# A running log-sum-exp kernel: weights marked as held, four loads up front, and a last store cut into 5, 75 and 48 partitions

The kernel runs on one core of a Trainium2 chip. The metric is the device time of one execution in microseconds (us), as the median of several executions of the same program; lower is better.

## The reference

For `x` of shape (4, 4096, 4128), float32, the output is a running log-sum-exp along the second axis:

```python
out[:, 0, :] = x[:, 0, :]
for t in range(1, S):
    mx = np.maximum(out[:, t - 1, :], x[:, t, :])
    out[:, t, :] = mx + np.log(np.exp(out[:, t - 1, :] - mx) + np.exp(x[:, t, :] - mx))
```

270.5 MB are read and as many written.

## The kernel before

The rows of a batch are taken in steps of 384 (R = 3 rows on each of 128 partitions), and one step of 256 per batch. A step is loaded whole, goes through ACT (Exp), PE (triangular matmuls that form prefix sums, plus the carry) and ACT (Ln), and is stored whole. Steps are cut into four column chunks, and the chunks of successive steps are interleaved on the engines. Cut to what the change and the argument touch:

```python
    def mm(pt, w, rhs, start=False, stop=False):
        nc.tensor.matmul(pt, lhsT=w, rhs=rhs, start=start, stop=stop, skip_group_check=True)
    ...
        def load(self):
            full = xpool.tile([P, R, D], FP32, name="xt")      # bufs = 4
            ...
            nc.sync.dma_start(out=self.xt, in_=self.dram(x))

        def store(self):
            nc.sync.dma_start(out=self.dram(out), in_=self.xt)
    ...
        def head(self):
            ...
            for j in range(t.r):
                for s in range(0, CH, MM):
                    mm(pt[:, s:s + MM], excl if j else incl, self.e(j, s, s + MM), start=j == 0)
            ...
    ahead = bufs - 1
    for s in steps[:ahead]:
        s.load()
    ...
    for g in range(len(chunks) + R - 1):
        for d in range(R - 1, -1, -1):
            if 0 <= g - d < len(chunks) and d < chunks[g - d].t.r:
                k = chunks[g - d]
                k.stage(d)                       # Ln of row d, then the matmuls of row d + 1
                if k.c == last and d + 1 == k.t.r:
                    k.t.store()
                    if stored + ahead < len(steps):
                        steps[stored + ahead].load()
                    stored += 1
        if g + 2 < len(chunks):
            chunks[g + 2].exp()
        if g + 1 < len(chunks):
            chunks[g + 1].head()
```

The softmax here doesn't subtract the row's maximum and nothing guards it: scores larger than these inputs give would overflow.

Of the kernel before, what the change touches and what calls it, by code (L numbers as in the profile page):

```python
# [10 lines left out]
P = 128  # L11
R = 3
CH = 1024
MM = 512
HI, LO = 96, 32


def _constants(nc, pool):


    def tri(base, name):
        t = pool.tile([P, P], FP16, name=name)
        nc.gpsimd.memset(t, 1.0)

        nc.gpsimd.affine_select(  # L25
            out=t, in_=t, pattern=[[1, P]], compare_op=mybir.AluOpType.is_ge,
            fill=0.0, base=base, channel_multiplier=-1,
        )
        return t

    def ones_where_zero(bases, step, name):
        t = pool.tile([P, P], FP16, name=name)
        nc.gpsimd.memset(t, 0.0)
        for base in bases:
            nc.gpsimd.affine_select(  # L35
                out=t, in_=t, pattern=[[step, P]], compare_op=mybir.AluOpType.not_equal,
                fill=1.0, base=base, channel_multiplier=1,
            )
        return t

    return (
        tri(0, "incl"),
        tri(-1, "excl"),
        ones_where_zero([0], -1, "ident"),
        ones_where_zero([-(HI + 31), -(LO + 31)], 0, "pick"),
    )


@with_exitstack
def kernel(  # L50
    ctx: ExitStack,
    tc: tile.TileContext,
    x: bass.AP,
    out: bass.AP,
):






    nc = tc.nc
    B, S, D = x.shape
    assert S % P == 0
    n_main = D // CH
    tail = D - n_main * CH
    t0 = n_main * CH
    last = n_main - 1

    nc.scalar.preload_act_table_set("natural_log_exp_and_others")  # L70
    consts = ctx.enter_context(tc.tile_pool(name="consts", bufs=1))
    incl, excl, ident, pick = _constants(nc, consts)

    bufs = 4
    xpool = ctx.enter_context(tc.tile_pool(name="xpool", bufs=bufs))
    cpool = ctx.enter_context(tc.tile_pool(name="cpool", bufs=1))
    pmain = ctx.enter_context(tc.tile_pool(name="pmain", bufs=3, space=bass.MemoryType.PSUM))
    ptail = ctx.enter_context(tc.tile_pool(name="ptail", bufs=2, space=bass.MemoryType.PSUM))

    carry = [cpool.tile([P, CH], FP16, name=f"carry{c}") for c in range(n_main)]  # L80
    carry_t = cpool.tile([P, tail], FP16, name="carry_t")
    for t in (*carry, carry_t):
        nc.vector.memset(t, 0.0)  # L83

    ctx.enter_context(tc.manual_schedule())

    def mm(pt, w, rhs, start=False, stop=False):
        nc.tensor.matmul(pt, lhsT=w, rhs=rhs, start=start, stop=stop, skip_group_check=True)  # L88

    def keep(cr, pt):  # L90

        nc.vector.tensor_copy(cr[HI:HI + 32, :], pt[HI:HI + 32])  # L92
        nc.vector.tensor_tensor(  # L93
            out=cr[LO:LO + 32, :], in0=pt[HI:HI + 32], in1=cr[HI:HI + 32, :],
            op=mybir.AluOpType.subtract,
        )

    class Step:


        def __init__(self, b, row, r):
            self.b, self.row, self.r = b, row, r
            self.first = row == 0

        def dram(self, t):
            rows = t[self.b, self.row:self.row + P * self.r, :]
            return rows.rearrange("(p j) d -> p j d", j=self.r)

        def load(self):
            full = xpool.tile([P, R, D], FP32, name="xt")  # L110
            self.xt = full[:, :self.r, :]
            self.half = self.xt.bitcast(FP16)
            nc.sync.dma_start(out=self.xt, in_=self.dram(x))  # L113

        def store(self):
            nc.sync.dma_start(out=self.dram(out), in_=self.xt)  # L116

    class Chunk:
        def __init__(self, step, c):
            self.t, self.c = step, c  # L120
            self.w = D - last * CH if c == last else CH

        def e(self, j, a, b):
            return self.t.half[:, j, 2 * self.c * CH + a:2 * self.c * CH + b]

        def exp(self):
            c0, w = self.c * CH, self.w
            nc.scalar.activation(  # L128
                self.t.half[:, :, 2 * c0:2 * c0 + w], self.t.xt[:, :, c0:c0 + w], ACT.Exp,
            )  # L130

        def head(self):
            t = self.t
            pt = self.pt = pmain.tile([P, CH], FP32, name="pt")
# [3 lines that stand above are left out]
            if not t.first:  # L138
                for s in range(0, CH, MM):
                    mm(pt[:, s:s + MM], pick, carry[self.c][:, s:s + MM])  # L140
            if self.c == last:
                self.tail_head()

        def tail_head(self):


            t, r = self.t, self.t.r
            full = ptail.tile([P, R, tail], FP32, name="qt")
            qt = self.qt = full[:, :r, :]
            to = lambda v, n: v.unsqueeze(1).to_broadcast([P, n, tail])  # L150
            for i in range(r):
                e = self.e(i, CH, CH + tail)
                mm(qt[:, i:, :], incl, to(e, r - i), start=i == 0)
                if i:
                    mm(qt[:, :i, :], excl, to(e, i))
            if not t.first:
                mm(qt, pick, to(carry_t, r))

        def stage(self, j):

            t, c, pt = self.t, self.c, self.pt
            nc.scalar.activation(t.xt[:, j, c * CH:(c + 1) * CH], pt, ACT.Ln)  # L162
            if j + 1 < t.r:
                for s in range(0, CH, MM):
                    mm(pt[:, s:s + MM], ident, self.e(j + 1, s, s + MM), stop=j + 2 == t.r)
                if c == last and j == 0:
                    nc.scalar.activation(t.xt[:, :, t0:D], self.qt, ACT.Ln)  # L167
                    keep(carry_t, self.qt[:, t.r - 1, :])
            else:
                keep(carry[c], pt)  # L170

    steps = []
    for b in range(B):
        n = S // P
        parts = [R] * (n // R) + ([n % R] if n % R else [])
        if b == 0:
            parts.reverse()
        row = 0
        for r in parts:
            steps.append(Step(b, row, r))  # L180
            row += P * r
        assert row == S

    chunks = [Chunk(s, c) for s in steps for c in range(n_main)]
    ahead = bufs - 1
    for s in steps[:ahead]:
        s.load()
    stored = 0
    chunks[0].exp()
    chunks[1].exp()  # L190
    chunks[0].head()
# [3 lines that stand above are left out]
                k = chunks[g - d]  # L195
                k.stage(d)
                if k.c == last and d + 1 == k.t.r:
                    k.t.store()
                    if stored + ahead < len(steps):
                        steps[stored + ahead].load()  # L200
                    stored += 1
        if g + 2 < len(chunks):
# [3 lines that stand above are left out]
# [30 lines left out]
```

## Time and profile before

| | before |
|---|---|
| time, median of the first 3 runs | 1262.91 us (1262.84 to 1263.04) |
| span of the profiled run | 1261.0 us |
| data queue, share of the 16 DMA engines' time | 99.4% |
| PE / weight loads / DVE / ACT busy | 55 / 19 / 36 / 75% |
| last load landed | 1220.69 us |
| last store: first packet starts, last packet ends | 1249.15, 1259.74 us |

The busy shares say what could be the bound, the chain of waits says what was at the end. Two things come from the packet records of the trace, which hold start, duration and size of every DMA packet: the duration of a packet, and which packets follow each other on one engine (the next starts a few ns before or after the last ends). The prediction below shows the other views.

### The profile page before, as it was taken

How to read it: one execution, taken by the hardware profiler on the slowest of the kernel's cores; microseconds unless marked ns; L12 is line 12 of the kernel's file. 1: busy time of each engine (PE TensorE's matmuls, PEld its weight loads, DVE VectorE, ACT ScalarE, POOL GpSimd, SP SyncE). 2: the span in 40 equal slices, each digit the busy share in tenths (PEclk: the TensorE clock that was granted, in tenths of full speed). 3: DMA queues.
4: the chain of work that ended last, by engine and by line, in shares of the span. 5: the costliest groups of instructions: out<-in, count | busy, mean ns of one | idle time of the engine just before them, and what ended most of it. 6: DMA issues, size and time to landing. Idle time of an engine off the chain costs nothing.

```text
span 1261.0 us, 6165 instructions
## 1 busy us (share of the span) xinstructions
PE 688.7 (55%) x2268; PEld 237.0 (19%) x2268; DVE 451.4 (36%) x445; ACT 947.3 (75%) x733; POOL 2.2 (0%) x13
## 2 busy tenths in 40 slices
PE   3665554555555555655346555555634755664552
PEld 1222111111121111211112211111211211221120
DVE  2443333333333333334424333333442433333344
ACT  5997777777777777778569777777966977777794
POOL 0000000000000000000000000000000000000000
PEclk9887777777677777777768777787777777778786
DMA  9999999999999999999999999999999999999998
GB/s 411 410 439 431 432 427 434 438 430 432 433 437 431 432 432 436 432 427 436 431 433 436 437 429 431 436 436 432 430 434 435 432 431 432 434 435 431 433 422 347
DMA packets 12702, 541.46 MB, mean 429 GB/s; under 512 B 1408, under 2 KB 1408, under 8 KB 1408
## 3 DMA queue, kind: packets, MB, share of 16 engines
q1 hardware_dynamic: 12672, 541.07, 99.4%
q8 instruction: 18, 0.29, 0.1%
q14 instruction: 12, 0.10, 0.0%
HBM read 270.53 MB, written 270.53 MB: 429 GB/s over the span
## 4 chain that ended last, share of the span: by engine, by line
DMA 69%; ACT 21%; PE 5%; issue 2%; DVE 1%; SPq 0%; ACTq 0%
DMA xt<-in_x_dram 67%; ACT xt L128 11%; ACT xt L162 10%; PE pt L88 5%; DMA out_dram<-xt 2%; ACT xt L167 0%; SPq L116 0%; DVE carry L92 0%; DVE carry L93 0%; ACTq L231 0%; SPq L113 0%; ACTq L128 0%; PE qt L88 0%
## 5 line engine op out<-in xcount | busy, mean ns | idle before, releaser
L128 ACT ACTIVATE xt<-xt 128x3072 f16<-128x3072 f32 (+3 forms) x176 | 478.5, 2719 | 247.9 <-DMA xt<-in_x_dram 247.8
L88 PE MATMUL pt<-xt,ident 128*128 128x512 f16 x672 | 251.3, 470 | 530.7 <-ACT xt L162 530.4
L162 ACT ACTIVATE xt<-pt 128x1024 f32<-128x1024 f32 x512 | 487.6, 1030 | 2.5 <-PE pt L88 0.7
L92 DVE CAST carry<-pt 32x1024 f16<-32x1024 f32 x176 | 216.4, 1230 | 761.0 <-ACT xt L162 760.7
L88 PE MATMUL pt<-xt,excl 128*128 128x512 f16 x672 | 247.0, 504 | 0.0
L93 DVE TENSOR_TENSOR carry<-pt,carry 32x1024 f16<-32x1024 f32 x176 | 215.9, 1227 | 6.1
L88 PEld LDWEIGHTS <-ident 128*128 128x128 f16 x672 | 70.1, 104 | 677.7 <-issue 654.0
L88 PE MATMUL pt<-xt,incl 128*128 128x512 f16 x352 | 152.0, 526 | 23.6 <-ACT xt L128 15.0
L88 PEld LDWEIGHTS <-excl 128*128 128x128 f16 x756 | 92.5, 124 | 141.0 <-issue 108.1
L88 PE MATMUL pt<-carry,pick 128*128 128x512 f16 x320 | 109.8, 429 | 0.0
L88 PEld LDWEIGHTS <-incl 128*128 128x128 f16 x480 | 45.2, 111 | 129.7 <-DVE carry L93 95.2
L88 PEld LDWEIGHTS <-pick 128*128 128x128 f16 x360 | 40.6, 113 | 57.0 <-issue 34.3
L167 ACT ACTIVATE xt<-qt 128x96 f32<-128x96 f32 (+1 forms) x44 | 10.9, 249 | 45.7 <-PE pt L88 45.7
L92 DVE CAST carry_t<-qt 32x32 f16<-32x32 f32 x44 | 8.7, 197 | 25.5 <-ACT xt L167 25.4
L88 PE MATMUL qt<-xt,incl 128*128 128x64 f16 (+2 forms) x128 | 12.3, 196 | 0.0
L88 PE MATMUL qt<-xt,excl 128*128 128x64 f16 (+1 forms) x84 | 10.6, 187 | 0.0
L93 DVE TENSOR_TENSOR carry_t<-qt,carry_t 32x32 f16<-32x32 f32 x44 | 8.5, 193 | 1.5
L88 PE MATMUL qt<-carry_t,pick 128*128 128x96 f16 (+1 forms) x40 | 8.2, 204 | 0.0
L83 DVE MEMSET carry<- 128x512 uint32 x4 | 1.9, 485 | 1.1 <-PEq L220 1.0
L70 ACT ACT_TABLE_LOAD x1 | 1.3, 1283 | 0.8 <-PEq L220 0.8
L35 POOL TENSOR_SCALAR_AFFINE_SELECT pick<-pick 128x128 f16<-128x128 f16 x2 | 0.6, 294 | 0.1
L25 POOL TENSOR_SCALAR_AFFINE_SELECT incl<-incl 128x128 f16<-128x128 f16 x1 | 0.3, 294 | 0.0
(11 smaller groups left out, 1.9 us busy)
## 6 DMA issues: line engine op xcount, KB each, us to landing
xt<-in_x_dram SPq DMA_DIRECT2D x40, 6192.0 KB, 42.2
out_dram<-xt SPq DMA_DIRECT2D x40, 6192.0 KB, 28.1
xt<-in_x_dram SPq DMA_DIRECT2D x4, 4128.0 KB, 37.3
out_dram<-xt SPq DMA_DIRECT2D x4, 4128.0 KB, 23.0
```

The lines of the kernel that those rows point to most:

```text
L25: nc.gpsimd.affine_select(out=t, in_=t, pattern=[[1, P]], compare_op=mybir.AluOpType.is_ge, fill=0.0, base=base, channel_multiplier=-1,)
L35: nc.gpsimd.affine_select(out=t, in_=t, pattern=[[step, P]], compare_op=mybir.AluOpType.not_equal, fill=1.0, base=base, channel_multiplier=1,)
L70: nc.scalar.preload_act_table_set("natural_log_exp_and_others")
L83: nc.vector.memset(t, 0.0)
L88: nc.tensor.matmul(pt, lhsT=w, rhs=rhs, start=start, stop=stop, skip_group_check=True)
L92: nc.vector.tensor_copy(cr[HI:HI + 32, :], pt[HI:HI + 32])
L93: nc.vector.tensor_tensor(out=cr[LO:LO + 32, :], in0=pt[HI:HI + 32], in1=cr[HI:HI + 32, :], op=mybir.AluOpType.subtract,)
L128: nc.scalar.activation(self.t.half[:, :, 2 * c0:2 * c0 + w], self.t.xt[:, :, c0:c0 + w], ACT.Exp,)
L162: nc.scalar.activation(t.xt[:, j, c * CH:(c + 1) * CH], pt, ACT.Ln)
L167: nc.scalar.activation(t.xt[:, :, t0:D], self.qt, ACT.Ln)
```

## The change

Three parts. First, a matmul whose stationary operand is the same as that of the matmul before it is to run without loading it again (`ldweights=False`), and the matmuls of the tail are put in an order that allows this more often. Second, all four buffers are loaded before the first store, in place of three. Third, the last store goes out as partitions 0-4, 5-79 and 80-127; the aim is that the fifth DMA engine, taken for the slow one, gets 4 packets of it and not 8.

```diff
--- before.py
+++ after.py
@@ -12,6 +12,9 @@
 R = 3
 CH = 1024
 MM = 512
+
+
+UNEVEN = ((0, 5), (5, 80), (80, P))
 HI, LO = 96, 32
 
 
@@ -84,8 +87,22 @@
 
     ctx.enter_context(tc.manual_schedule())
 
+    held = [None]
+
     def mm(pt, w, rhs, start=False, stop=False):
-        nc.tensor.matmul(pt, lhsT=w, rhs=rhs, start=start, stop=stop, skip_group_check=True)
+
+        if held[0] is not w:
+            nc.tensor.matmul(pt, lhsT=w, rhs=rhs, start=start, stop=stop, skip_group_check=True)
+            held[0] = w
+            return
+        pe = nc.tensor
+        pe.add_instruction(mybir.InstMatmult(
+            name=nc.get_next_instruction_name(),
+            ins=[pe.lower_ap(rhs), pe.lower_ap(w, for_matmul_weights=True)],
+            outs=[pe.lower_ap(pt, opt=True)],
+            start_tensor_calc=start, stop_tensor_calc=stop, ldweights=False,
+            tile_size=(P, P), tile_position=(0, 0), bass_skip_group_check=True,
+        ))
 
     def keep(cr, pt):
 
@@ -112,8 +129,9 @@
             self.half = self.xt.bitcast(FP16)
             nc.sync.dma_start(out=self.xt, in_=self.dram(x))
 
-        def store(self):
-            nc.sync.dma_start(out=self.dram(out), in_=self.xt)
+        def store(self, parts=((0, P),)):
+            for a, b in parts:
+                nc.sync.dma_start(out=self.dram(out)[a:b], in_=self.xt[a:b])
 
     class Chunk:
         def __init__(self, step, c):
@@ -149,10 +167,9 @@
             qt = self.qt = full[:, :r, :]
             to = lambda v, n: v.unsqueeze(1).to_broadcast([P, n, tail])
             for i in range(r):
-                e = self.e(i, CH, CH + tail)
-                mm(qt[:, i:, :], incl, to(e, r - i), start=i == 0)
-                if i:
-                    mm(qt[:, :i, :], excl, to(e, i))
+                mm(qt[:, i:, :], incl, to(self.e(i, CH, CH + tail), r - i), start=i == 0)
+            for i in range(1, r):
+                mm(qt[:, :i, :], excl, to(self.e(i, CH, CH + tail), i))
             if not t.first:
                 mm(qt, pick, to(carry_t, r))
 
@@ -183,7 +200,7 @@
 
     chunks = [Chunk(s, c) for s in steps for c in range(n_main)]
     ahead = bufs - 1
-    for s in steps[:ahead]:
+    for s in steps[:bufs]:
         s.load()
     stored = 0
     chunks[0].exp()
@@ -195,8 +212,8 @@
                 k = chunks[g - d]
                 k.stage(d)
                 if k.c == last and d + 1 == k.t.r:
-                    k.t.store()
-                    if stored + ahead < len(steps):
+                    k.t.store(UNEVEN if k.t is steps[-1] else ((0, P),))
+                    if bufs <= stored + ahead < len(steps):
                         steps[stored + ahead].load()
                     stored += 1
         if g + 2 < len(chunks):
```

## The prediction

> **What bounds the kernel now.** I read the page first, the DMA part before the engine part, then the chain of waits in its last 80 us, then the order of instructions on SP and ACT there.
>
> ```profile
> PE 688.7 (55%) x2268; PEld 237.0 (19%) x2268; DVE 451.4 (36%) x445; ACT 947.3 (75%) x733; POOL 2.2 (0%) x13
> ...
> DMA packets 12702, 541.46 MB, mean 429 GB/s; under 512 B 1408, under 2 KB 1408, under 8 KB 1408
> ...
> q1 hardware_dynamic: 12672, 541.07, 99.4%
> q8 instruction: 18, 0.29, 0.1%
> q14 instruction: 12, 0.10, 0.0%
> ```
>
> The data queue keeps the 16 DMA engines busy for 99.4% of the span; no compute engine is above 75%. 12672 packets are 88 transfers (44 loads, 44 stores) of 128 data packets, one per partition, and 16 completion writes. Each engine gets 8 data packets of each transfer. In the packet records a 49,536-byte packet takes 1.829 us and a 33,024-byte one 1.222 us, in nearly every case: 27 GB/s per engine, loads and stores alike. An engine therefore needs 8 x (80 x 1.829 + 8 x 1.222) = 1248.8 us of the 1261.0; successive packets overlap by 3 to 4 ns, 704 times, so about 1246. Nothing in the change takes a byte away. What can move is the other 15 us: the start, the places where an engine stands still, and the tail.
>
> Chaining packets (the next starts 3 to 4 ns before the last ends) gives 16 engine histories. They start at 1.8 to 2.4 us. One never stops and ends at 1259.74; the other 15 end at 1258.9 to 1259.1. The span ends 1.3 us after the last packet. Those 15 stood still once, before the next-to-last store:
>
> ```profile
> SPq L116 <- ACT xt L162: 1178.4, 44, 30.0
> ```
> ```profile
> 1183.04 37.65 DMA xt<-in_x_dram
> 1220.69 0.02 issue
> ...
> 1220.78 1.91 ACT xt L128
> 1222.68 2.75 ACT xt L162 x3
> ...
> 1225.48 0.61 PE pt L88 x2
> ...
> 1226.11 0.25 ACT xt L167
> 1226.36 1.80 ACT xt L128
> 1228.16 2.74 ACT xt L162 x3
> 1230.90 1.11 ACT xt L128
> ```
> ```profile
> DMA  9299949994979779472402021200920092009202
> ```
>
> SP issues a store only after the ACT work of its step, and ACT runs exponentials of the next step in between. So the next-to-last store waits for the last load, landed at 1220.69, plus 12.9 us of nearly gapless ACT work, and is issued at 1233.63. The DMA digits (1221 to 1240 us, 0.48 us each) show the engines running dry one after another from about 1228 and starting together near 1235. Then 8 packets of 1.829 and 8 of 1.222 us give 24.3 us, to 1259. The last store, issued at 1244.12, has about 5 us in hand. The end is thus set twice over: by the last load's landing on the *slowest* engine, and by that engine's own unbroken backlog.
>
> Why one engine is slow is in the landings. The 16 completions of the first load lie within 0.54 us, those of the last within 7.3 us (next slowest 6.2, then 4.6; mean about 2.9). The packet histories show one cause: the 16-KB instruction fetches of queue q8, 18 of them some 65 us apart, each landing on one engine and delaying it by about 1.5 us (a gap near 1.0 and a stretched packet near 0.45, for example at 59, 604 and 1101 us). The 8-KB ones cost about 0.6.
>
> [...]
>
> **The change, part by part.**
>
> *Held weights.* A three-block chunk has 12 matmuls in the order ident (4), incl (2), excl (4), pick (2), each preceded by a load; held, 4 loads remain. The tail chunk has 6 more matmuls, 3 more loads after the reordering. Per step 3 x 4 + 7 = 19 loads in place of 54; in all about 820 in place of 2268. PE is not the bound, so the 1450 loads at 0.11 us (160 us) are nearly all worth nothing. Two pieces are on the path. First, in the last chain ACT waits once for a pair of ident matmuls (0.61 us)[...]. Second, the program shrinks [...], so q8 goes from 18 fetches to 12 or 13. Five or six delays of 1.5 us over 16 engines are 0.5 us on average, but what counts is the slowest engine, whose lag contains two or three fetches: one fewer is 1.5 us, none fewer is 0, two fewer 3. I choose 1.5. It brings the last landing, the next-to-last store and the end forward by as much.
>
> *Four loads up front.* The fourth load was issued at 37.39, right behind the first store at 37.00; now it is before it. The rings held work until 42 us in both cases, and from the load of step 4 on the order of transfers is the same. Same bytes, no gap filled: 0. One oddity could pay: the last packets of the third load, at 40 us, took 2.5 to 3.2 us in place of 1.829 on all engines. If that is because the rings were nearly empty when the first store arrived, it goes, 1.1 us; if it belongs to the first store as such, it only moves. The last store also met a short queue (5 us) without such a packet, so I give it one in five: minus 0.2.
>
> *The last store in three.* Partitions 5, 75 and 48 run on 5, 15 and 16 engines with 1, 5 and 3 packets each. That the fifth engine gets 4 (1 + 3) is true only if a transfer's engines start where the last one's left off: the 75 then use all but the fifth. Engines one to four get 9, the rest 8. [...] Either way some engines carry 9 packets, 1.222 us more. They were ready at 1259.0, so they end at 1260.2 where the slowest ended at 1259.74: plus 0.5. If the fifth is the slow one, its 4 packets spare it 4.9 us, of which only the 0.74 by which it trails can be of use. Two more issues on SP (0.34 us each) fit into the 5 us in hand; two more completion writes of 9 ns are nothing.
>
> Sum: 0.5 - 1.5 - 0.15 - 0.2 = -1.35, and 1262.91 - 1.35 = 1261.6.
>
> **Rivals.**
>
> (a) The slowest engine's lag does not shrink: other engines lose the fetches, or the lag is not from fetches. For it: its lag also crept up by about 0.15 us per pair of transfers from 5.06 at 820 us to 7.3, with no fetch. Then only +0.5 - 0.15 remains: about 1263.3. If the slowest engine is also among the nine-packet ones it is 1262.9 + 1.2 - 0.15 = 1264.
>
> (b) The lag halves, the 40-us packet goes too: 0.5 - 3.5 - 0.15 - 1.1, near 1258.7. Against it: most engines show two fetches in the whole run, so losing two on one engine is the exception.
>
> (c) A faster PE speeds up the whole. ACT idles 45.7 us behind PE (44 waits before the small tail logarithm)[...]. Against it: ACT also stands 247.8 us waiting for loads; what it saves earlier it waits longer for DMA. Only the wait in the last chain is on the path.
>
> (d) The partial stores are slower per packet, or the 5-partition one holds up the rest. At 33,024 B per packet nothing should change; if the first ran alone before the others, 1.2 us: about 1263.
>
> **Range and chances.** The three runs before lie within 0.2 us, so the width comes from the landing of a dozen fetches and from which engines get nine packets: 1259.6 to 1263.3 covers (a), (c), (d) and most of (b). 2% are 25 us, more than the whole 15 us that do not move data; so within 2% is nearly certain: 0.99, and 0.005 on each side.
>
> **What would show it.** Right: q8 at 12 or 13; weight loads near 820; the spread of the last load's landings down from 7.3 to 5 to 6 us and the landing 1 to 2 us earlier; the next-to-last store issued 12.7 us after it; the last packets on nine-packet engines ending 1.2 us after the eight-packet ones. Wrong: a spread still above 7 us; a long packet at the first store gone; the engine with few packets not being the one that trailed; a data queue under 99% anywhere before 1220 us.

The term of 0.15, the estimate for a pair of ident matmuls without its second load, rests on no run.

The 12 or 13 fetches can be had from the page as an estimate: 18 fetches for 2268 matmuls and 2268 weight loads are one for 252 of these instructions, so 1450 fewer would save 5.8. That q8 follows the PE program is measured below: 12 fetches with 1344 of these instructions fewer (e7_fewer), 26 with 2268 more (e9_more). The 5, 15 and 16 engines are also those of the changed kernel's trace (36 completion writes); of the two counts of packets that it gave, one is the one that this trace shows: 9 on five engines, 8 on ten, 3 on one. Two figures are measured: the groups of weight loads take 104 to 124 ns in the mean, and the slices of the page lie at 427 to 439 GB/s, but for the first two (411, 410) and the last two (422, 347).

## The result, and the profile after

The changed kernel takes 1272.06 us (1271.59 to 1272.38, 6 runs), the kernel before 1262.95 us (1262.84 to 1263.08) in the same rounds. The ratio is 1.0072, 95% interval 1.0059 to 1.0085: 9.1 us more, outside the predicted range. A ratio here and below is the mean time of one kernel's runs over that of the other's of the same rounds, so not quite the ratio of the medians that are quoted.

The page of the changed kernel, engines and DMA queues:

```profile
PE 687.0 (54%) x2268; PEld 236.2 (19%) x2268; DVE 451.4 (36%) x445; ACT 947.5 (75%) x733; POOL 2.2 (0%) x13
...
DMA packets 12722, 541.46 MB, mean 426 GB/s; under 512 B 1428, under 2 KB 1428, under 8 KB 1428
...
q1 hardware_dynamic: 12692, 541.07, 99.0%
q8 instruction: 18, 0.29, 0.1%
```

There are 2268 weight loads as before, and 18 fetches on q8. The held weights removed nothing. The groups of the page say where the loads come from; line 99 is the branch of `mm` that adds the matmul with `ldweights=False`:

```profile
L99 PEld LDWEIGHTS <-ident 128*128 128x128 f16 x496 | 50.9, 103 | 657.7 <-issue 643.9
L99 PEld LDWEIGHTS <-excl 128*128 128x128 f16 x536 | 66.6, 124 | 103.3 <-issue 78.7
```

With the incl (260) and pick (160) loads of that line, 1452 loads ran for matmuls that were marked to go without; the other 816 are those of line 95, which are meant to load. So this part of the change had no effect on the chip; why the mark had none stays open. The data queue has 20 packets more: 36 completion writes for the last store in place of 16, which is 5 + 15 + 16.

The chain of waits, in order of time, around the last load (start, duration, what):

```profile
1183.68 37.65 DMA xt<-in_x_dram
1221.37 0.04 issue
1221.41 1.91 ACT xt L146
1223.32 2.75 ACT xt L179 x3
...
1226.11 0.60 PE pt L99 x2
...
1226.74 0.25 ACT xt L184
```

The last load lands at 1221.33 us, 0.64 later than before; the wait for two ident matmuls is still 0.60 us. Up to here nothing is won and little lost. The loss is behind it. Stretches of the last store, as the table by time windows gives them, first of the kernel before, then of the changed one (the last two columns are the mean number of packets in flight per DMA engine, as a share, and GB/s):

```profile
1250.00:1259.00 9.00, 0.00 (x0) 0.00 (x0) 0.00 (x0) 0.00 (x0) 0.00 (x0) 0.50 0.95 411
```
```profile
1251.00:1259.00 8.00, 0.00 (x0) 0.00 (x0) 0.00 (x0) 0.00 (x0) 0.00 (x0) 0.50 0.80 285
1259.00:1268.00 9.00, 0.00 (x0) 0.00 (x0) 0.00 (x0) 0.00 (x0) 0.00 (x0) 0.50 0.42 158
```

No engine computes any more, and the store moves 285 and then 158 GB/s where it moved 411. In the first stretch the DMA engines are 80% busy and yet carry only two thirds of the rate: packets take longer. In the second fewer than half have work. In the packet records the last store runs from 1249.81 to 1269.07 us, 19.3 us, and before from 1249.15 to 1259.73, 10.6 us. That is 8.7 of the 9.3 us by which the last packet ends later in the profiled runs; the other 0.65 is the later start.

Six of the sixteen engine histories of this store in the changed kernel, by chaining the packets (us of each data packet, s a completion write). Some of the others cross in places and are left out; the last line, the engine that ends last, can be followed too, and the same history stands in the trace of e2_split below (6.89, 2.81):

```
1.22 1.22 1.22 s                                           end 1253.58   3 data packets
2.48 2.56 1.90 1.65 1.26 s 2.41 1.22 1.22 s                end 1264.51   8
7.13 s 1.22 1.22 1.22 1.22 1.22 s 1.22 1.22 1.22 s         end 1266.75   9
7.28 s 1.22 1.22 1.22 1.22 1.22 s 1.22 1.22 1.22 s         end 1267.05   9
7.48 s 1.22 1.22 1.22 1.22 1.22 s 2.84 1.22 1.22 s         end 1268.80   9
6.89 s 1.22 1.22 1.22 1.22 1.22 s 2.84 1.22 1.22 s         end 1269.07   9
```

Two things are new here. Packets that took 1.222 us in the kernel before take up to 7.5; four of the five packets of the first transfer took 6.9 to 7.5 us and the fifth 1.22. And the counts are 9 (1 + 5 + 3) on five engines, 8 (5 + 3) on ten, and 3 on one. The trace does not number the engines, but every engine that the first part used got nine packets, and none got four.

### The profile page after: what moved, and what is told of

Read it like the earlier page. It is cut to its first block, busy times and chain, and to the rows that moved or that the text cites. A ratio compares the mean times of both kernels' runs of the same rounds, so it can differ in the third digit from the quotient of the medians.

```text
span 1270.5 us, 6167 instructions
## 1 busy us (share of the span) xinstructions
PE 687.0 (54%) x2268; PEld 236.2 (19%) x2268; DVE 451.4 (36%) x445; ACT 947.5 (75%) x733; POOL 2.2 (0%) x13
## 4 chain that ended last, share of the span: by engine, by line
DMA 71%; ACT 19%; PE 4%; issue 2%; DVE 1%; SPq 0%; ACTq 0%
DMA xt<-in_x_dram 67%; ACT xt L146 10%; ACT xt L179 9%; DMA out_dram<-xt 4%; PE pt L99 3%; PE pt L95 2%; DVE carry L109 0%; DVE carry L110 0%; ACT xt L184 0%; SPq L134 0%; ACTq L248 0%; SPq L130 0%; ACTq L146 0%; PE qt L95 0%
## 5 line engine op out<-in xcount | busy, mean ns | idle before, releaser
L95 PE MATMUL pt<-xt,ident 128*128 128x512 f16 x176 | 77.0, 438 | 497.1 <-ACT xt L179 497.1
L99 PE MATMUL pt<-xt,ident 128*128 128x512 f16 x496 | 202.9, 477 | 36.0 <-ACT xt L179 35.7
L99 PE MATMUL pt<-xt,excl 128*128 128x512 f16 x496 | 186.6, 495 | 0.0
L95 PE MATMUL pt<-xt,incl 128*128 128x512 f16 x176 | 91.6, 520 | 23.6 <-ACT xt L146 15.0
L95 PE MATMUL pt<-xt,excl 128*128 128x512 f16 x176 | 92.4, 525 | 0.0
L99 PE MATMUL pt<-xt,incl 128*128 128x512 f16 x176 | 92.3, 525 | 0.0
L95 PE MATMUL pt<-carry,pick 128*128 128x512 f16 x160 | 71.8, 449 | 0.0
L99 PE MATMUL pt<-carry,pick 128*128 128x512 f16 x160 | 67.9, 424 | 0.0
L95 PEld LDWEIGHTS <-incl 128*128 128x128 f16 x220 | 22.8, 104 | 118.2 <-DVE carry L110 95.0
L99 PEld LDWEIGHTS <-incl 128*128 128x128 f16 x260 | 27.9, 116 | 11.5 <-issue 6.1
```

Source lines behind the costliest of these rows:

```text
L99: pe.add_instruction(mybir.InstMatmult(name=nc.get_next_instruction_name(), ins=[pe.lower_ap(rhs), pe.lower_ap(w, for_matmul_weights=True) ...
```

## The experiments

The theory after the result: the loss is the split alone, and it comes from which partitions a transfer covers. A transfer over partitions 0-63, 64-127, 0-31 or 96-127 alone would run at half rate, so that a packet of 1.222 us takes 2.44; one over 32-95, or over all 128, at full rate. The expectations call this the port theory; the reason for it is shown by no run. What follows tests the forecast, not the reason. The rivals: something in the first two parts of the change; the uneven packet counts; or a fixed cost of each further transfer at the end.

**e1_whole** undoes the split in the changed kernel, **e2_split** puts only the split into the kernel before.

```diff
# e1_whole, against the changed kernel
-                    k.t.store(UNEVEN if k.t is steps[-1] else ((0, P),))
+                    k.t.store()
# e2_split, against the kernel before
-                    k.t.store()
+                    k.t.store(((0, 5), (5, 80), (80, P)) if k.t is steps[-1] else ((0, P),))
```

> The changed kernel with its last store whole again. Split theory (the 9.1 us come from the three-part last store alone): 1263.0, within 0.7 us of the kernel before. Rival 1 (the four early loads or the reordered tail matmuls shift all work): stays above 1268.

> The kernel before with only its last store split 5, 75, 48. Split theory: 1271 to 1273, as the changed kernel. Rival 1: 1262.9 to 1264.

Measured: e1_whole 1262.73 us (ratio 1.0, 0.9985 to 1.0015), e2_split 1271.55 us (ratio 1.0072, 1.0056 to 1.0087), both beside 1262.68 for the kernel before. The split is the whole of the loss, and the other two parts together are worth nothing that these runs can tell. In e1_whole the profile has 2268 weight loads, as in the changed kernel.

**e3_halves** cuts the last store of the kernel before into partitions 0-63 and 64-127, **e4_mixed** into 32-95, 0-31 and 96-127.

```diff
# against the kernel before; e4_mixed has ((32, 96), (0, 32), (96, P))
-                    k.t.store()
+                    k.t.store(((0, 64), (64, P)) if k.t is steps[-1] else ((0, P),))
```

> Last store as partitions 0-63 and 64-127: every engine has 4 + 4 packets, no engine has nine. Port theory [...]: packets near 2.44 us, last store 19.6 us in place of 9.8, total 1272.5 to 1273. Rival 2 (uneven packet counts, nine on some engines, three on one): 1262.9 to 1263.3, packets at 1.222 us.

> Last store as partitions 32-95, 0-31, 96-127: engines have 4 + 2 + 2 packets. Port theory: [...] 4 packets of 1.222 us each; the other two [...] 2 packets of 2.44 us each; together 14.7 us, total near 1267.8. Rival 2: 1263. Rival 3 (each further transfer in the last store costs something fixed; 9.1 us for two more, so 4.5 for one): here 1272 and the halves 1267.5, the other way round from the port theory.

Measured: e3_halves 1272.76 us (ratio 1.008, 1.0063 to 1.0096), e4_mixed 1267.58 us (1.0039, 1.0024 to 1.0054). Both are where the port theory put them. Every engine has eight packets in both, so uneven counts are not the cause; and two transfers cost twice what three cost, so it is not a price per transfer. Engine histories, three of e3_halves and three of e4_mixed:

```
2.42 2.57 2.57 2.63 s 1.22 2.57 2.57 2.57 s                e3_halves
2.38 2.57 2.57 2.75 s 1.56 2.57 2.57 2.58 s
2.54 2.57 2.57 2.55 s 2.53 2.57 2.57 2.02 s
1.22 1.22 1.22 1.22 s 2.38 2.60 s 2.11 2.52 s              e4_mixed
1.22 1.22 1.22 1.22 s 2.51 2.55 s 2.52 2.16 s
1.22 1.22 1.22 1.22 s 2.63 2.53 s 2.54 2.09 s
```

The time windows of e3_halves, then of e4_mixed (its first transfer, then its other two):

```profile
1251.00:1259.00 8.00, 0.00 (x0) 0.00 (x0) 0.00 (x0) 0.00 (x0) 0.00 (x0) 0.50 0.98 198
1261.00:1268.00 7.00, 0.00 (x0) 0.00 (x0) 0.00 (x0) 0.00 (x0) 0.00 (x0) 0.50 1.07 226
```
```profile
1251.00:1254.00 3.00, 0.00 (x0) 0.00 (x0) 0.00 (x0) 0.00 (x0) 0.00 (x0) 0.50 1.13 484
1256.00:1259.00 3.00, 0.00 (x0) 0.00 (x0) 0.00 (x0) 0.00 (x0) 0.00 (x0) 0.50 0.88 176
1259.00:1263.00 4.00, 0.00 (x0) 0.00 (x0) 0.00 (x0) 0.00 (x0) 0.00 (x0) 0.50 1.09 264
```

All engines are busy in all five stretches (a packet is counted where it starts, so a short stretch can show over 1.00). What differs is the rate: 198 and 226 GB/s for partitions 0-63 and 64-127, full rate for 32-95 (484 in a short stretch, 411 for the store of the kernel before), and 176 and 264 GB/s, about half, for 0-31 and 96-127. The first transfers of e3_halves and e4_mixed have the same size, 64 neighbouring partitions, the same number of engines and packets, and the same spacing in DRAM; only the partitions differ, and the packets take 2.57 and 1.22 us. That points to the SBUF side. The addresses in DRAM differ as well, by 32 rows of the store; a run with the same addresses and other partitions was not made.

**e5_rows** keeps three transfers, but each over all 128 partitions.

```diff
-            nc.sync.dma_start(out=self.dram(out), in_=self.xt)
+            o, h = self.dram(out), D // 2
+            if self is not steps[-1]:
+                nc.sync.dma_start(out=o, in_=self.xt)
+                return
+            nc.sync.dma_start(out=o[:, 0, :], in_=self.xt[:, 0, :])
+            nc.sync.dma_start(out=o[:, 1, :h], in_=self.xt[:, 1, :h])
+            nc.sync.dma_start(out=o[:, 1, h:], in_=self.xt[:, 1, h:])
```

> Last store in three transfers again, but each of all 128 partitions: row 0, then row 1 in two column halves. Port theory: [...] 24 packets of half or quarter size per engine, total 1262.5 to 1263.5. Rival 3 (three transfers as such cost 9 us): 1272.

Measured: 1263.54 us beside 1262.70 (ratio 1.0006, 0.9989 to 1.0022), a little over the upper end of what was expected but far from 1272. Three transfers as such cost 0.8 us at the most; in its profile the last load had landed 0.6 us later already.

**e6_loads** is the kernel before with only the four loads up front.

```diff
-    for s in steps[:ahead]:
+    for s in steps[:bufs]:
-                    if stored + ahead < len(steps):
+                    if bufs <= stored + ahead < len(steps):
```

> The kernel before with only the four loads up front. Both theories of the prediction: 1262.9, within 0.7 us. The stretched packets at 40 us move to the first store, near 54 us (if the first store causes them), or vanish and give 1.1 us (if the short queue does).

Measured: 1262.75 us beside 1262.70 (ratio 1.0, 0.9985 to 1.0015). The stretched packets moved: in its packet records they stand at 54 to 55 us on all 16 engines (0.7 to 1.4 us too long), just ahead of the first store, as in the changed kernel. They belong to the first store, not to a short queue.

**e7_fewer** asks what held weights would have been worth if they had worked. It leaves out the excl matmuls of the chunk heads, so that the PE program is about as short as it should have become. Its output is wrong, which doesn't matter for the time.

```diff
-            for j in range(t.r):
+            for j in range(1):
                 for s in range(0, CH, MM):
                     mm(pt[:, s:s + MM], excl if j else incl, self.e(j, s, s + MM), start=j == 0)
```

> The kernel before without the excl matmuls of the chunk heads: 672 matmuls and 672 weight loads fewer, wrong result on purpose. It gives the instruction stream the size that held weights should have given (12 to 13 fetches on q8). Fetch theory of the prediction: the last load's spread falls from 7.3 us to 5 to 6 and the time by 1.5 us, to 1261.4. Rival (the slowest engine's lag is not from fetches): 1262.9, within 0.4 us.

Measured: 1261.63 us (1261.48 to 1261.77) beside 1262.70 (1262.62 to 1262.94). The ratio 0.9991 has an interval of 0.9978 to 1.0005, which includes 1, but no run of one kernel reaches into the range of the other. The page, and the chain at the last load:

```profile
q8 instruction: 12, 0.20, 0.1%
```
```profile
1181.85 37.61 DMA xt<-in_x_dram
...
1219.54 1.91 ACT xt L128
```

Twelve fetches; the landings of the last load spread over 6.2 us in place of 7.3, and the last of them is at 1219.45 in place of 1220.69. So 1.1 us, not the 1.5 of the prediction, and where it was expected, at the last landing. (The traces with 18 fetches and the same work up to there have spreads of 6.8 to 7.4 us and last landings from 1220.57 to 1221.67, so the shift of the landing in this one trace is no larger than what varies without it; the times above are the firmer evidence.) The run also takes 30% of the matmuls from PE, and its granted clock was 0.65 in place of 0.77. The wait of ACT for the ident matmuls on the last chain grew (1.10 us, before 0.68), so the gain does not come from there. That it comes from the fetches and from nothing else that the removal changed is likely, not isolated.

**e8_early** tests the claim that the end is set twice over. It cuts the last two stores by columns, so that their first halves go out as soon as their chunks are done.

```diff
-        def store(self):
-            nc.sync.dma_start(out=self.dram(out), in_=self.xt)
+        def store(self, a=0, b=D):
+            nc.sync.dma_start(out=self.dram(out)[:, :, a:b], in_=self.xt[:, :, a:b])
...
+                if k.t in steps[-2:] and k.c == 1 and d + 1 == k.t.r:
+                    k.t.store(0, 2 * CH)
                 if k.c == last and d + 1 == k.t.r:
-                    k.t.store()
+                    k.t.store(2 * CH if k.t in steps[-2:] else 0)
```

> The kernel before with the two last stores cut by columns, so that half of each goes out some 10 us and 5 us earlier: the 4 us in which 15 engines stood still should fill. If the end is set by the unbroken backlog of the slowest engine as well (the prediction's claim), the time stays near 1262.9 or falls by at most 0.7 us; if the next-to-last store's issue alone sets it, it falls by 3 to 5 us.

Measured: 1263.60 us beside 1262.70 (ratio 1.0007, 0.9992 to 1.0022): no gain. The DMA digits of e8_early from 1221 to 1240 us, and from 1240 to 1261:

```profile
DMA  9979977999797929993889799898999989999999
```
```profile
DMA  9999999899899899989989999767653311100000
```

The hole of the kernel before is gone, and the engines now run out one after another at the end, over 7.3 us in the landings of the last transfer. The fifteen faster ones are done early; the slowest ends at 1260.22 us, no earlier than before. Its backlog is a bound of its own. The cut by columns also turns 16 packets of an engine into 40 of 0.309 us and 40 of 0.315 us, by these durations 0.3 to 0.5 us more (an estimate); that is part of the 0.9 us lost, and too little to hide a gain of 3 to 5.

**e9_more** is a dose the other way: one more weight load ahead of each matmul.

```diff
+        nc.tensor.ldweights(w)
         nc.tensor.matmul(pt, lhsT=w, rhs=rhs, start=start, stop=stop, skip_group_check=True)
```

> The kernel before with one more weight load ahead of every matmul: 2268 PE instructions more, 26 to 27 fetches on q8 in place of 18. From the run with 12 fetches (6 fewer: 1.07 us less) the fetch theory expects 8 or 9 more to cost about 1.5 us, total 1264.2, with a wider spread of the last load's landings. Rival (the run with fewer matmuls was faster because PE had less to do on the last chain): the doubled loads also slow PE there, but the q8 count would not matter and the landing of the last load would not move.

Measured: 1267.07 us beside 1262.86 (ratio 1.0033, 1.0020 to 1.0047), with 26 fetches and a spread of 8.3 us. The direction is that of the fetch theory, the size is nearly three times what it gave. In the profile the last load lands 3.6 us later, at 1224.27. About 1.1 us of the packet time per engine are packets stretched on many engines at once near 914, 930, 999 and 1014 us, which the kernel before does not have; what causes them stays open. As evidence for the size of a fetch this run is inconclusive.

## Why the prediction was wrong

- **The last store in three: this step failed.** The prediction took 1.222 us per packet whatever the partitions ("at 33,024 B per packet nothing should change") and so came to one further packet on some engines, plus 0.5 us. The term measures 8.7 us. What the runs show in its place is that the time of a packet depends on the partitions that are written at the same time. With 0-63 or 64-127 alone most packets take about 2.57 us (e3_halves), with 32-95 alone 1.22 (e4_mixed). The split 5, 75, 48 loses as much in another way. Of the first transfer four packets took 6.9 to 7.5 us and one 1.22. The engine that ends last spends 5.7 us more on its first packet than 1.22, 1.6 on another long one, and 1.2 on its ninth: 8.5 of the 8.7 us. After the first packet most of its packets take 1.22, so this is not the halves' doubling of every packet. The two packets of 2.84 us, one on each of the two engines that end last, are not explained here, and no run put five other partitions in the first part, so why four of its packets are slow is not shown.
- **Rival (d), and the counts.** The prediction did name the danger that partial stores are slower per packet, and dismissed it with the packet's size. It was right that the counts of the change's intent need not hold: five engines got nine packets, one got three. The ninth packet costs the 1.2 us that the prediction gave it.
- **Held weights: failed.** 820 loads and 12 or 13 fetches were forecast; there were 2268 and 18. The prediction believed the flag. The forecast gain of 1.5 us therefore never came; with the 12 fetches of e7_fewer the time was 1.1 us less. The 0.15 us from a shorter pair of ident matmuls, the estimate, did not come either (0.61 us before, 0.60 after).
- **Four loads up front: right.** 0 was forecast and 0 measured. The stretched packets moved to the first store, the case given four chances in five.
- **The bound: right.** The end is set both by the last load's landing on the slowest engine and by that engine's backlog: e7_fewer moved both, with fewer fetches; e8_early filled the hole and won nothing.
- **A small slip of the working.** The stated range began at 1259.6 us and so did not reach the 1258.7 of rival (b).

No experiment gave a correct kernel that is faster than the kernel before beyond the spread of its runs. How to take work from the slowest engine without slowing its packets was not tried.

## What to carry to other kernels

When a transfer is cut by partitions, look at how long the packets of each part take, not only at how many each DMA engine has to move: here 32-95 ran at 1.22 us a packet, 0-63 at 2.57, and the five partitions 0-4 held four engines for some 7 us. A cut of the last store by rows and columns, each part over all 128 partitions, cost 0.8 us at the most (e5_rows). Check that an option took effect before counting its gain; here the number of weight loads on the first page says that it did not. In this kernel, whose data queue fills 99.4% of the DMA engines' time, the length of the instruction stream is likely a cost, though a small one: six fetches fewer went with 1.1 us less (e7_fewer).
